# Gate chunks of the in-projection in pairs by seven quarter products, their tanh through DRAM, projections by output feature

## Chip, cores and metric

One core of one Trainium2 chip. The metric is the device time of one launch in microseconds (us): 1536.8 us, the median of 3 runs (1535.43 to 1537.21).

## What is computed

Two layers of a decoder trunk over 1024 prompt rows and 8 sample rows, 1032 in all. Cut to what matters here, each layer does, in fp32:

```
h = x @ w_in                          # (1032, 1024) @ (1024, 5632)
xa, za, u, v, zb, q, k, vv, zc, gates = split(h)
ya = pool_mix(xa) * silu(za)          # 256 features
yb = u * sgu(layer_norm(v)) * silu(zb)   # 256
yc = window_attention(rope(q), rope(k), vv) * silu(zc)   # 512
merged = sum over i of sigmoid(gates_i + b_gate_i) * (y_i @ w_proj_i)   # i = a, b, c; 1024 each
x = layer_norm(ALPHA * x + merged @ w_out)
```

Every product is made of three fp32r products of high and low parts: x_h w_h + x_l w_h + x_h w_l.

## The kernel before

x lies in SBUF by feature as XH and XL (8 slices of 128 features by 1032 rows). A chunk is 128 output features of the in-projection. `unit(w, s)` (line 584) makes a third of a chunk (384, 384 or 264 rows): 8 slices by 3 terms, 24 matmuls into one of 4 PSUM banks (`acc`). What follows reads that bank: tanh on ScalarE (ACT), arithmetic on VectorE (DVE). The weights of the next chunk are loaded by SP and split meanwhile (`prep_chunk`, line 184): ACT copies the high part `wh`, DVE subtracts the low part `wl` (`split`, lines 92 to 94).

The order within a layer is written out in lines 920 to 996: rows of v (`a0`), five rotary chunks (`rope`), chunks 0 to 3 of the pool branch (`b_chunk`), eight gate chunks of branch a (`c_chunk(0, d)`), chunks 4 to 11 (branch b, and four chunks of the attention's gate zc), eight gate chunks each of b and c, then the output projection with layer norm by blocks of rows (`d_mm`, `d_ln`, `d_tr`). In a `c_chunk` the projection of its branch is done right there, by `merge` (line 753): for each third it multiplies y and w_proj into a bank of `att`, and DVE makes `(tanh + 1) * product` and adds it to `mg[d]`. Each third's merge comes one unit after its gate.

The attention is cut into steps (`att_query`, `att_scores`, `att_norm`, `att_tr`, `att_pv`) that a list hands out between matmuls: `Jobs.pump` (line 48) is called every six matmuls, and starts a step that uses TensorE at most every 1.45 calls.

Each engine runs its own instructions in the order in which the program issues them, and an instruction that waits holds up those behind it.

Of the kernel before, what the change touches and what calls it, by code (L numbers as in the profile page):

```python
# [16 lines left out]
L = 2  # L17
S = 1024
# [9 lines left out]
class Jobs:  # L28
    def __init__(self):
        self.tick = 0  # L30
        self.lists = [deque(), deque(), deque()]
        self.at = {}
        self.free = 0
# [13 lines left out]

    def pump(self):
        self.tick += 1
        for i in (0, 2, 1):  # L50
            q = self.lists[i]
            while q and all(k in self.at and self.tick >= self.at[k] + lag for k, lag in q[0][2]):
                if i == 1 and self.tick < self.free:
                    break
                if self._run(q):
                    if i == 1:
                        self.free = max(self.free, self.tick - 1) + 1.45
                    return

# [10 lines left out]
class Feed:  # L70
    """Raw weights, loaded in the order in which they are split."""

    def __init__(self, nc, new, items, first=()):
        self.nc, self.new, self.items, self.raw = nc, new, deque(items), deque()
        self.first = deque(first)

    def stage(self):
        if self.items:
            src = self.items.popleft()
            n = src.free_size()  # L80
            t = self.first.popleft() if self.first else self.new()
            self.nc.sync.dma_start(out=t[:, 0:n], in_=src)
            self.raw.append((t, n))

    def take(self, use, stage=True):
        t, n = self.raw.popleft()
        use(t[:, 0:n])
        if stage:
            self.stage()
# [8 lines left out]
def trunk_kernel(  # L98
    ctx: ExitStack,
    tc: tile.TileContext,  # L100
    xb, xs, xp, xst, wA, wB, wC, wP, wPc, wO, lcol, lrow, kcT, ck, cv, hist, ln, tab, c_a, c_b,
# [8 lines left out]
    wrp = ctx.enter_context(tc.tile_pool(name="wrp", bufs=2))  # L110
    wlp = ctx.enter_context(tc.tile_pool(name="wlp", bufs=2))
    whp = ctx.enter_context(tc.tile_pool(name="whp", bufs=2))
    prp = ctx.enter_context(tc.tile_pool(name="prp", bufs=1))
    plp = ctx.enter_context(tc.tile_pool(name="plp", bufs=2))
    php = ctx.enter_context(tc.tile_pool(name="php", bufs=2))
# [6 lines left out]

    def t_acc():
        return acc.tile([128, 512], F32, tag="acc", name="acc")
# [4 lines left out]
    def t_w2():  # L129
        return w2.tile([128, 512], F32, tag="w2", name="w2")  # L130
# [4 lines left out]
    def t_m(j, dt=F32R, name="m", n=T):  # L135
        return big.tile([128, n], dt, tag=f"m{j}", name=f"{name}{j}")
# [3 lines left out]

    def t_q(j, dt=F32R, n=T, name="q"):
        return big.tile([128, n], dt, tag=f"q{j}", name=f"{name}{j}")

    def t_r(j, dt=F32R, n=T, name="r"):
        return big.tile([128, n], dt, tag=f"r{j}", name=f"{name}{j}")
# [5 lines left out]
    x2d.append(drm.tile([NS, DM], F32, name="x2ds"))  # L151

# [9 lines left out]
    def order():  # L162
        for l in range(L):
            yield from [wA[l, :, k:k + 2] for k in (0, 2, 4, 6)]
            yield from [wB[l, j] for j in range(9)]
            yield from [wC[l, 0, d] for d in range(8)]
            yield from [wB[l, j] for j in range(9, 17)]
            yield from [wC[l, 1, d] for d in range(8)]
            yield from [wC[l, 2, d] for d in range(5)]
            yield wO[l, 0, :, 0:2]  # L170
            yield wC[l, 2, 5]
            yield wO[l, 0, :, 2:4]
            yield from [wC[l, 2, d] for d in range(6, 8)]
            yield from [wO[l, 0, :, k:k + 2] for k in (4, 6)]
            yield from [wO[l, 1, :, k:k + 2] for k in (0, 2, 4, 6)]

    def proj_order():
        for l in range(L):
            yield from [wP[l, i, d] for i in range(2) for d in range(4)]
            yield from [wPc[l, d] for d in range(8)]  # L180

    wq, pq_, half_done = deque(), deque(), []

    def prep_chunk(m=None, parts=2):
        """Splits the next raw chunk, or one half of it."""
        if not half_done:
            raw, n = feed.raw.popleft()
            if m is None:
                h = whp.tile([128, 1024], F32R, tag="wh", name="wh")
                lo = wlp.tile([128, 1024], F32R, tag="wl", name="wl")  # L190
            else:
                h, lo = [t_m(m + i, name="wm")[:, 0:1024] for i in range(2)]
            half_done.append((h, lo, raw))
            wq.append((h, lo))
            cs = slice(0, 1024 if parts == 2 else 512)
        else:
            h, lo, raw = half_done[0]
            cs = slice(512, 1024)
        split(nc, h[:, cs], lo[:, cs], raw[:, cs])
        if cs.stop == 1024:  # L200
            half_done.pop()
            feed.stage()

    def prep_proj():
        def use(raw):
            h = php.tile([128, 512], F32R, tag="ph", name="ph")
            lo = plp.tile([128, 512], F32R, tag="pl", name="pl")
            split(nc, h, lo, raw)
            pq_.append((h, lo))
        if pfeed.raw:  # L210
            pfeed.take(use)

    class Slices:
        """One group of columns of a weight of 1024 rows: per 128 rows, its high and its low part."""

        def __init__(self, where, cols=512):
            self.h, self.lo, self.n, self.where, self.cols = {}, {}, 0, where, cols

        def prep(self, n=4, stage=True):
            for _ in range(n):  # L220
                if self.n < 4:
                    feed.take(self._pair, stage)

        def _pair(self, raw):
            k0, n = 2 * self.n, self.cols
            if self.where == "p" and k0 == 0:
                self.p = t_p(name="slp")
            if self.where == "p" and k0 >= 4:
                h = whp.tile([128, 1024], F32R, tag="wh", name="slh")[:, 0:2 * n]
                lo = wlp.tile([128, 1024], F32R, tag="wl", name="sll")[:, 0:2 * n]  # L230
                split(nc, h, lo, raw)
                for j in range(2):
                    self.h[k0 + j], self.lo[k0 + j] = h[:, j * n:j * n + n], lo[:, j * n:j * n + n]
            else:
                for j in range(2):
                    k = k0 + j
# [75 lines left out]
    class Layer:  # L312
# [38 lines left out]
        def rope(self, j):  # L351
            w = wq.popleft()
            cos, sin = self.tab
            for s in range(3):
                p, e, n = self.unit(w, s)
                if s < 2 and j != 1:
                    prep_chunk(parts=1)
# [243 lines left out]
        def b_chunk(self, j):  # L601
            w = wq.popleft()
            for s in range(3):
# [15 lines left out]
                if s < 2:  # L619
                    prep_chunk(parts=1)  # L620
# [480 lines left out]
```

## Time and profile before

| | |
|---|---|
| median of 3 runs | 1536.8 us |
| span of the profiled execution | 1535.0 us (the three runs lie 0.4 to 2.2 us above it) |
| TensorE matmul (PE) busy | 1514.7 us, 99% |
| VectorE (DVE) | 733.3 us, 48% |
| ScalarE (ACT) | 494.9 us, 32% |
| GpSimd (POOL) | 212.3 us, 14% |
| DMA | 63 GB/s on average, 96.65 MB |

The page shows the span of one execution; its own time outside the span isn't shown. Matmuls are pipelined: one of 384 columns is shown as some 340 ns, while the next starts 175 ns after it. So the steps between starts, and not the durations, make up the time of TensorE.

### The profile page before, as it was taken

Reading aid. Unit: us, or ns where it says so; the run is one execution under the profiler, and the core shown is the slowest. Engines: PE = TensorE matmul, PEld = TensorE weight load, DVE = VectorE, ACT = ScalarE, POOL = GpSimd, SP = SyncE. Lnnn points to the kernel's source line nnn. Section 1 sums busy time; section 2 is a strip of 40 time slices with the busy share of each in tenths; the row PEclk is TensorE's granted clock in tenths of the full one; section 3 lists DMA queues with packets and bytes.
Section 4 is the critical chain, followed back from the end, with each engine's and each line's share of the span. In section 5 each row is a group of like instructions: output and inputs, shape, how many; then the busy total and the mean of one; then the engine's idle time right before and its main releaser. Section 6 shows DMA issues by size and latency. Waiting matters only on the chain.

```text
span 1535.0 us, 23080 instructions
## 1 busy us (share of the span) xinstructions
PE 1514.7 (99%) x9344; PEld 1432.1 (93%) x9344; DVE 733.3 (48%) x1726; ACT 494.9 (32%) x1163; POOL 212.3 (14%) x300
## 2 busy tenths in 40 slices
PE   8999999999999999999999999999999999999997
PEld 8998899999999999988799988999999999999876
DVE  6347755424433333364863477554243333332647
ACT  4454555421222212140215545554212222122300
POOL 4523110000000000001565231100000000000015
PEclk9999999999999999999999999999999999999999
DMA  6311111111111112233413111111111111121313
GB/s 228 114 52 31 35 44 35 35 49 32 52 50 42 48 44 67 62 104 97 139 69 128 47 36 30 37 34 42 42 42 42 56 49 35 56 63 49 120 59 124
DMA packets 43418, 96.65 MB, mean 63 GB/s; under 512 B 8864, under 2 KB 14032, under 8 KB 43280
## 3 DMA queue, kind: packets, MB, share of 16 engines
q1 hardware_dynamic: 33232, 86.16, 17.4%
q10 hardware_dynamic: 10080, 9.03, 1.7%
q8 instruction: 73, 1.20, 0.3%
q14 instruction: 33, 0.27, 0.1%
HBM read 86.14 MB, written 11.11 MB: 63 GB/s over the span
## 4 chain that ended last, share of the span: by engine, by line
PE 46%; DVE 3%; ACT 1%; issue 0%; POOL 0%; DVEq 0%; POOLq 0%; ACTq 0%
PE acc L591 29%; PE acc L295 7%; PE att L761 6%; PE att L489 1%; PE att L448 1%; PE att L478 1%; PE acc L301 1%; ACT w L456 0%; DVE w L468 0%; PE att L720 0%; DVE rr L839 0%; DVE rr L842 0%; DVE sll L94 0%; POOL rr L843 0%; DVE py L690 0%
## 5 line engine op out<-in xcount | busy, mean ns | idle before, releaser
L591 PE MATMUL acc<-XH,wh 128*128 128x384 f32 (+1 forms) x1872 | 611.9, 327 | 0.0
L591 PE MATMUL acc<-XL,wh 128*128 128x384 f32 (+1 forms) x1872 | 598.5, 320 | 0.0
L591 PE MATMUL acc<-XH,wl 128*128 128x384 f32 (+1 forms) x1872 | 598.5, 320 | 0.0
L591 PEld LDWEIGHTS acc<-XH,wh 128*128 128x128 f32 x1872 | 352.4, 188 | 14.0 <-issue 12.5
L591 PEld LDWEIGHTS acc<-XL,wh 128*128 128x128 f32 x1872 | 352.7, 188 | 1.2
L591 PEld LDWEIGHTS acc<-XH,wl 128*128 128x128 f32 x1872 | 352.1, 188 | 0.0
L94 DVE TENSOR_TENSOR wl<-wr,wh 128x512 fp32r<-128x512 f32 x156 | 109.2, 700 | 289.1 <-ACT wh L93 288.8
L776 ACT ACTIVATE w<-acc,halves 128x384 f32<-128x384 f32 x144 | 78.5, 545 | 411.2 <-PE acc L591 411.2
L284 POOL TENSOR_TENSOR rr<-rr,mhalf 128x1 f32<-128x1 f32 (+1 forms) x18 | 10.3, 572 | 959.7 <-DVE rr L283 959.7
L93 ACT ACTIVATE wh<-wr 128x512 fp32r<-128x512 f32 x156 | 97.0, 624 | 27.0 <-PE acc L591 19.5
L456 ACT ACTIVATE w<-w,ns 128x256 f32<-128x256 f32 (+1 forms) x128 | 62.4, 488 | 116.9 <-DVE ns L454 116.9
L295 PE MATMUL acc<-slp,XH 128*128 128x384 f32 (+1 forms) x256 | 73.7, 371 | 5.8 <-ACT slp L93 5.8
L765 DVE SCALAR_TENSOR_TENSOR w<-w,att 128x384 f32<-128x384 f32 (+1 forms) x96 | 48.9, 510 | 37.6 <-PE att L761 37.6
L361 ACT ACTIVATE w<-acc 32x384 f32<-32x384 f32 (+1 forms) x120 | 53.9, 449 | 36.1 <-PE acc L591 33.3
L761 PE MATMUL att<-ycl,ph 128*128 128x384 f32 (+1 forms) x192 | 61.5, 320 | 0.0
L761 PE MATMUL att<-ych,pl 128*128 128x384 f32 (+1 forms) x192 | 61.4, 320 | 0.0
L761 PE MATMUL att<-ych,ph 128*128 128x384 f32 (+1 forms) x192 | 61.2, 319 | 0.0
L295 PEld LDWEIGHTS acc<-slp,XH 128*128 128x128 f32 x256 | 47.9, 192 | 11.7 <-ACT slp L93 5.8
L454 DVE CUSTOM_DVE_ANT_0 w<-att,cb,skn 128x256 f32<-128x256 f32 (+1 forms) x128 | 54.7, 465 | 8.6 <-PE att L448 6.8
L94 DVE TENSOR_TENSOR pl<-pr,ph 128x512 fp32r<-128x512 f32 x32 | 22.1, 692 | 68.3 <-ACT ph L93 68.3
L598 ACT ACTIVATE w<-acc 128x384 f32<-128x384 f32 (+1 forms) x48 | 21.8, 455 | 93.9 <-PE acc L591 93.9
L766 DVE TENSOR_TENSOR mg<-mg,w 128x384 f32<-128x384 f32 (+1 forms) x96 | 49.6, 516 | 3.3
(205 smaller groups left out, 2241.8 us busy)
## 6 DMA issues: line engine op xcount, KB each, us to landing
wr<-in_wC_dram SPq DMA_DIRECT2D x48, 512.0 KB
wr<-in_wB_dram SPq DMA_DIRECT2D x34, 512.0 KB
wr<-in_wO_dram SPq DMA_DIRECT2D x16, 512.0 KB
pr<-in_wP_dram SPq DMA_DIRECT2D x16, 256.0 KB
pr<-in_wPc_dram SPq DMA_DIRECT2D x16, 256.0 KB
w<-in_xp_dram SPq DMA_DIRECT2D x16, 256.0 KB
x2d<-rr ACTq DMA_DIRECT2D x16, 256.0 KB
w<-x2d SPq DMA_DIRECT2D x16, 256.0 KB
```

The costliest lines, as they stand in the source:

```text
L93: nc.scalar.activation(h, raw, AF.Copy)
L94: nc.vector.tensor_tensor(lo, raw, h.bitcast(F32), op=ALU.subtract)
L295: PE.matmul(p[:, 0:n], x[:, k, blk(b)], c, start=(i == 0 and j == 0), stop=(i == len(terms) - 1 and j == len(t) - 1))
L361: A.activation(t[a:a + 32, 0:n], p[b:b + 32], AF.Copy)
L454: V.tensor_tensor_reduce(o, ps[:, i * 256:i * 256 + w], mask[:, m0:m0 + w], 1.0, self.c["skn"][:, j:j + 1], op0=ALU.add, op1=ALU.min, accu ...
L456: A.activation(o, o, AF.Exp, bias=nm[:, i:i + 1], scale=-1.0, accum_out=su[:, i:i + 1])
L591: PE.matmul(p[:, 0:n], a[:, c], b[:, k, o:o + n], start=(k == 0 and j == 0), stop=(k == 7 and j == 2))
L598: A.activation(t[:, 0:n], p, AF.Tanh, scale=0.5)
L761: PE.matmul(q[:, 0:n], a[:, c], b[:, e], start=(k == 0 and j == 0), stop=(k == nk - 1 and j == 2))
L765: V.scalar_tensor_tensor(t[:, 0:n], t[:, 0:n], 1.0, q[:, 0:n], op0=ALU.add, op1=ALU.mult)
L766: V.tensor_tensor(m[:, e], m[:, e], t[:, 0:n], op=ALU.add)
L776: A.activation(t[:, 0:n], p, AF.Tanh, bias=self.c["h"][:, i * 8 + d:i * 8 + d + 1], scale=0.5)
```

## The change

**Products.** The 24 gate chunks and the 4 zc chunks are made in 14 pairs per layer (`pair`). The 1024 input features, the 256 output features of a pair and the 1032 rows are each cut in two halves, and the pair is seven products (the Winograd form of Strassen) of 512 features by 128 outputs by 516 rows, where eight would be the plain way. A product is 4 slices by 3 terms by 2 matmuls of 258 columns. The sums that it needs:

- of weights: 4 additions of 128 by 512 per pair on POOL (`first`, `second`);
- of x: T2, T3 and T4 of four slices each, by 44 additions of 128 by 516 per layer on POOL, and each of the 12 slices is split again by ACT and DVE (`queue_folds`, a fourth list of jobs, one per pump in which no TensorE step starts); a last sum overwrites half of XH and XL after chunk 7 (`fold_last`);
- of products: PSUM accumulates some, ACT makes one copy and DVE six additions of 516 per pair.

**Order.** Chunks 0 to 7 come first, then 12 gate pairs, 2 zc pairs, and then all projections (`project(d)`, for output features d = 0 to 7). The tanh of the gates goes to DRAM and comes back (`gd`), as do ya and yb (`yd`). All of y is split into high and low parts after the last pair.

**Buffers.** PSUM `acc` is 2 pairs of banks. Weight tiles are half as large (512 columns) and more (`wr` 6, `wh` and `wl` 4). The scratch tiles `w2` are 4 where they were 8, with 4 `ap` for the attention. The pace of attention steps is 2.6 calls.

The core of the diff:

```diff
-    w2 = ctx.enter_context(tc.tile_pool(name="w2", bufs=8))
-    acc = ctx.enter_context(tc.tile_pool(name="acc", bufs=4, space=PSUM))
+    stp = ctx.enter_context(tc.tile_pool(name="stp", bufs=3))
+    w2 = ctx.enter_context(tc.tile_pool(name="w2", bufs=4))
+    app = ctx.enter_context(tc.tile_pool(name="app", bufs=4))
+    acc = ctx.enter_context(tc.tile_pool(name="acc", bufs=2, space=PSUM))
...
+        def fold(self, k0, k1, dst, eng):
+            (a, ao), (b, bo) = k1, k0
+            h, lo = [t_st() if eng is None else t_w2()[:, 0:HT] for _ in range(2)]
+            eng = eng or G
+            eng.tensor_tensor(h, XH[:, a, ao:ao + HT].bitcast(F32), XH[:, b, bo:bo + HT].bitcast(F32), op=ALU.subtract)
+            eng.tensor_tensor(lo, XL[:, a, ao:ao + HT].bitcast(F32), XL[:, b, bo:bo + HT].bitcast(F32), op=ALU.subtract)
+            eng.tensor_tensor(dst, h, lo, op=ALU.add)
...
+            def t3(k):
+                r = t_st()
+                self.fold((k, HT), (k + 4, HT), r, None)
+                split(nc, *place(3, k), r)
+                return False
...
+            for k in range(4):
+                J.add(3, lambda k=k: t3(k), ("T3", k), [(("pool", 1), 2)])
+            for k in range(4):
+                J.add(3, lambda k=k: t2(k), ("T2", k))
+            for k in range(4):
+                J.add(3, lambda k=k: t4(k), ("T4", k), [(("ya", 1), 6)])
+
+        def fold_last(self):
+            for k in range(4):
+                r = t_w2()[:, 0:HT]
+                self.fold((k, 0), (k, HT), r, V if k % 2 else G)
+                split(nc, XH[:, k, HT:T], XL[:, k, HT:T], r)
...
+        def product(self, n, ps, first):
+            h, lo = ready.popleft()
+            for k in range(4):
+                c = slice(k * 128, k * 128 + 128)
+                xh, xl = self.quarter(n, k)
+                for j, (a, b) in enumerate(((h, xh), (h, xl), (lo, xh))):
+                    for s in range(2):
+                        PE.matmul(ps[:, s, 0:258], a[:, c], b[:, s * 258:s * 258 + 258],
...
+            A_, B_ = t_two(), t_two()
+            self.product(11, A_, True)
+            A.activation(v(lo1), ps(A_), AF.Copy)
+            self.product(2, B_, True)
+            add(hi0, lo1, B_)
+            self.product(21, A_, False)
+            use(0, 0, ps(A_))
+            self.product(3, B_, False)
+            add(hi1, lo1, B_)
+            C_ = t_two()
+            self.product(1, C_, True)
+            add(hi1, hi1, C_)
+            use(1, 1, v(hi1))
+            self.product(4, B_, False)
+            add(lo1, lo1, B_)
+            use(1, 0, v(lo1))
+            self.product(22, C_, False)
+            add(hi0, hi0, C_)
+            use(0, 1, v(hi0))
...
+                for q in range(2):
+                    ps = t_two()
...
+                    V.scalar_tensor_tensor(v(t), v(t), 1.0, ps[:, :, 0:258], op0=ALU.add, op1=ALU.mult)
+                    if i:
+                        (V if last else G).tensor_tensor(m[:, e], m[:, e], t[:, e], op=ALU.add)
+                    if i == 2:
+                        split(nc, XH[:, d, e], XL[:, d, e], m[:, e])
+                    if (i < 2 and q) or (i == 2 and not q and d >= 3):
+                        prep()
```

What this does to the order of instructions is shown at three places.

**ScalarE while x is summed** (layer 0, chunks 3 and 4). L598 and L615 are the tanh of a unit's bank, L93 and L94 the copies of high parts (of weights `wh`, of ya `yah`, of T3 and T2), L427 and L445 the attention's query, L456 and L474 its exponentials, L480 and L498 its copy of transposed rows. Before:

```order
L598 ACTIVATE w_1700<-acc 128x264 [waits PE_49]
L495 ACTIVATE yc<-att 128x4x128 [waits PE_49]
L480 ACTIVATE w_1740<-att 128x512 [waits PE_49]
L598 ACTIVATE w_1748<-acc 128x384 [waits PE_49]
L93 ACTIVATE wh<-wr 128x512 [waits DMAHW3_49]
L427 ACTIVATE ks_688<-yc 64x256
L456 ACTIVATE w_1765,ns<-w_1765,ns 128x256 [waits DVE_49] x2
L459 ACTIVATE ns<-ns 128x2 [waits DVE_49]
```

And now:

```order
L615 ACTIVATE w_1872<-acc 128x384 [waits PE_49]
L94 ACTIVATE wh<-wr 128x512 [waits DMAHW0_49]
L651 DMA yd_108<-yax_1155 128x1032 [waits DMAHW2_49,DVE_49]
L94 ACTIVATE T3x_1894<-st 128x516 [waits Pool_49]
L498 ACTIVATE ap<-att 128x512 [waits PE_49]
L94 ACTIVATE T3x_1894<-st 128x516 [waits Pool_49]
L94 ACTIVATE T2x_1943<-st 128x516 [waits Pool_49]
L615 ACTIVATE w_1947<-acc 128x384 [waits DVE_49,PE_49]
L94 ACTIVATE wh<-wr 128x512
L445 ACTIVATE ksu_734<-yc 64x256
L474 ACTIVATE ap,ns<-ap,ns 128x256 [waits DVE_49] x2
L477 ACTIVATE ns<-ns 128x2 [waits DVE_49]
L94 ACTIVATE T2x_1943<-st 128x516 [waits Pool_49]
L498 ACTIVATE ap<-att 128x512 [waits PE_49]
```

The copies of T3 and T2, each behind a wait for POOL, stand between the tanh of a unit and the attention's copies.

**ScalarE at the first pair** (layer 0). Before, at the end of chunk 3 and the first gate chunk (L776 is the gate's tanh):

```order
L93 ACTIVATE yah_1910<-ya_1109 128x384 [waits DVE_49,PE_49,Pool_49]
L93 ACTIVATE yah_1910<-ya_1109 128x384 [waits DVE_49]
L93 ACTIVATE yah_1910<-ya_1109 128x264 [waits DVE_49]
L480 ACTIVATE w_1936<-att 128x512 [waits PE_49]
L776 ACTIVATE w_1938<-acc,halves 128x384
L93 ACTIVATE wh<-wr 128x512 [waits DMAHW6_49]
L427 ACTIVATE ks_688<-yc 64x256
```

Now, from the end of chunk 7 (L651 sends yb to DRAM, the four L94 with `XH` are `fold_last`, L821 is the copy of product 11 which product 21 waits for):

```order
L651 DMA yd_110<-ybu_1832 128x1032 [waits DVE_49]
L94 ACTIVATE XH<-w_2560 128x516 [waits Pool_49]
L94 ACTIVATE XH<-w_2568 128x516 [waits DVE_49]
L94 ACTIVATE XH<-w_2576 128x516 [waits Pool_49]
L94 ACTIVATE XH<-w_2584 128x516 [waits DVE_49]
L94 ACTIVATE wh<-wr 128x512 [waits DMAHW6_49]
L498 ACTIVATE ap<-att 128x512 [waits PE_49]
L94 ACTIVATE wh<-wr 128x512
L445 ACTIVATE ksu_734<-yc 64x256
L474 ACTIVATE ap,ns<-ap,ns 128x256 [waits DVE_49] x2
L477 ACTIVATE ns<-ns 128x2 [waits DVE_49]
L821 ACTIVATE gu_2593<-acc 128x516 [waits PE_49]
```

The four copies of `fold_last` come first, in turns with POOL and DVE; the third weight tile of the pair and then the copy of product 11 stand behind them.

**VectorE in the projections** (layer 1 before, chunk by chunk; layer 0 now, d = 2). L763 to L766 and L907 multiply a product with its gate or add it up. Before:

```order
L765 SCALAR_TENSOR_TENSOR w_11838<-w_11838,att 128x384 [waits PE_49]
L766 TENSOR_TENSOR mg_9799<-mg_9799,w_11838 128x384 [waits DVE_49]
L94 TENSOR_TENSOR pl<-pr,ph 128x512 [waits DMAHW0_49,Activation_49]
L765 SCALAR_TENSOR_TENSOR w_11869<-w_11869,att 128x384 [waits PE_49]
L766 TENSOR_TENSOR mg_9799<-mg_9799,w_11869 128x384 [waits DVE_49]
L765 SCALAR_TENSOR_TENSOR w_11909<-w_11909,att 128x264 [waits PE_49]
L766 TENSOR_TENSOR mg_9799<-mg_9799,w_11909 128x264 [waits DVE_49]
```

Now:

```order
L907 SCALAR_TENSOR_TENSOR glu_6543<-glu_6543,acc 128x516 [waits DMAHW2_49,PE_49]
L907 SCALAR_TENSOR_TENSOR glu_6543<-glu_6543,acc 128x516 [waits PE_49]
L95 TENSOR_TENSOR wl<-wr,wh 128x512 [waits Activation_49]
L907 SCALAR_TENSOR_TENSOR glu_6615<-glu_6615,acc 128x516 [waits DMAHW5_49,DVE_49,PE_49]
L907 SCALAR_TENSOR_TENSOR glu_6615<-glu_6615,acc 128x516 [waits PE_49]
L95 TENSOR_TENSOR wl<-wr,wh 128x512 [waits Activation_49]
L907 SCALAR_TENSOR_TENSOR glu_6675<-glu_6675,acc 128x516 [waits DMAHW6_49,DVE_49,PE_49]
L95 TENSOR_TENSOR XL<-glu_6543,XH 128x516 [waits Activation_49]
L907 SCALAR_TENSOR_TENSOR glu_6675<-glu_6675,acc 128x516 [waits PE_49]
L95 TENSOR_TENSOR XL<-glu_6543,XH 128x516 [waits Activation_49]
```

The additions into `mg` have gone to POOL, and the split of XL, which waits for ACT and so for POOL, stands between the readers of two banks (rows 7 and 9) and ahead of those of the next d.

## Rows read from the trace of the kernel before

**Rows 1.** The page: span, busy time of the engines, clock in 40 slices.

```profile
span 1535.0 us, 23080 instructions
PE 1514.7 (99%) x9344; PEld 1432.1 (93%) x9344; DVE 733.3 (48%) x1726; ACT 494.9 (32%) x1163; POOL 212.3 (14%) x300
PEclk9999999999999999999999999999999999999999
```

**Rows 2.** Waits of TensorE, the longest: line, waited for; us in all, times, longest.

```profile
PE acc L295 <- ACT slp L93: 5.8, 1, 5.8
```

**Rows 3.** Chain that ended last: start, us, units of two gate chunks.

```profile
1237.97 8.41 PE acc L591 x48
1247.44 2.90 PE acc L591 x24
```

**Rows 4.** Timeline, TensorE: start, us; weight loads (PEld) and attention steps.

```profile
402.35 0.19 PEld L591 LDWEIGHTS acc<-XH,wl 128*128 128x128 f32 x1
...
206.56 0.60 PE L478 MATMUL att<-ident,w 128*128 128x128 f32 x4
206.91 0.37 PE L591 MATMUL acc<-XH,wh 128*128 128x264 f32 x1
...
207.73 0.64 PE L448 MATMUL att<-ks 128*128 128x256 f32 x4
208.20 0.29 PE L591 MATMUL acc<-XH,wh 128*128 128x264 f32 x1
```

**Rows 5.** Timeline, POOL: two-input additions of several widths.

```profile
91.07 1.01 POOL L364 TENSOR_TENSOR yc<-yc,w 128x384 f32<-128x384 f32 x1 [2.87 <-DVE w L363]
104.65 0.76 POOL L364 TENSOR_TENSOR yc<-yc,w 128x264 f32<-128x264 f32 x1 [1.25 <-DVE w L363]
137.28 1.89 POOL L666 TENSOR_TENSOR px<-xa 128x1024 f32<-128x1024 f32 x1
...
729.44 3.81 POOL L843 TENSOR_TENSOR rr<-rr,w 128x512 f32<-128x512 f32 x2 [1.77 <-issue]
735.53 2.87 POOL L843 TENSOR_TENSOR rr<-rr,w 128x512 f32<-128x512 f32 x2 [1.77 <-issue]
```

**Rows 6.** Groups by form, DVE, ACT and POOL: busy us, mean ns, idle before.

```profile
L94 DVE TENSOR_TENSOR wl<-wr,wh 128x512 fp32r<-128x512 f32 x156 | 109.2, 700 | 289.1 <-ACT wh L93 288.8
...
L94 DVE TENSOR_TENSOR ycl<-yc,ych 128x1032 fp32r<-128x1032 f32 x8 | 9.7, 1230 | 4.7 <-ACT ych L93 4.7
...
L93 ACT ACTIVATE wh<-wr 128x512 fp32r<-128x512 f32 x156 | 97.0, 624 | 27.0 <-PE acc L591 19.5 <-POOL vns L339 7.1
L93 ACT ACTIVATE ych<-yc 128x1032 fp32r<-128x1032 f32 x8 | 8.3, 1063 | 5.8 <-DVE yc L618 4.0 <-PE att L761 1.9
...
L420 POOL TENSOR_TENSOR ks<-kT,ks 64x128 fp32r<-64x128 f32 x64 | 32.6, 509 | 4.3
L418 POOL CAST ks<-kT 64x128 fp32r<-64x128 f32 x64 | 20.6, 322 | 170.6 <-PE att L448 168.1
```

**Rows 7.** Windows of the first 20 us: PE, PEld, DVE, ACT, POOL busy, clock, DMA, GB/s.

```profile
0.00:5.00 5.00, 0.00 (x0) 0.00 (x0) 0.38 (x2) 1.91 (x2) 0.20 (x4) 1.00 0.60 167
5.00:10.00 5.00, 4.15 (x12) 3.79 (x13) 4.35 (x7) 4.16 (x8) 0.00 (x0) 1.00 1.03 386
10.00:15.00 5.00, 5.00 (x26) 5.00 (x25) 3.02 (x7) 2.35 (x4) 0.55 (x1) 1.00 1.03 389
15.00:20.00 5.00, 5.00 (x30) 5.00 (x30) 3.23 (x10) 1.46 (x3) 3.20 (x4) 1.00 1.03 419
```

**Rows 8.** Timeline, TensorE, the first block of rows.

```profile
10.45 0.52 PE L295 MATMUL acc<-sll,XH 128*128 128x384 f32 x1
10.77 0.52 PE L295 MATMUL acc<-slh,XL 128*128 128x384 f32 x1
...
11.68 0.34 PE L295 MATMUL acc<-slh,XL 128*128 128x384 f32 x1
11.86 0.33 PE L295 MATMUL acc<-slh,XH 128*128 128x384 f32 x1
```

More of the change, by code (lines that the diff above doesn't have):

```diff
@@ L17 @@
 L = 2
+HT = 516
 S = 1024
@@ L46, in _run, with _ready @@
         return pe is not False
+    def _ready(self, q):
+        return q and all(k in self.at and self.tick >= self.at[k] + lag for k, lag in q[0][2])
     def pump(self):
@@ L51, in pump @@
             q = self.lists[i]
-            while q and all(k in self.at and self.tick >= self.at[k] + lag for k, lag in q[0][2]):
+            while self._ready(q):
                 if i == 1 and self.tick < self.free:
@@ L70, with __init__, stage @@
 class Feed:
-    def __init__(self, nc, new, items, first=()):
+    def __init__(self, nc, new, items):
         self.nc, self.new, self.items, self.raw = nc, new, deque(items), deque()
[L75 to L89, printed above, removed]
+    def stage(self, n=1):
+        for _ in range(n):
+            if self.items:
+                src = self.items.popleft()
+                c = src.free_size()
+                t = self.new()[:, 0:c]
+                self.nc.sync.dma_start(out=t, in_=src)
+                self.raw.append(t)
 def split(nc, h, lo, raw):
@@ L121, in trunk_kernel, with t_two @@
     ctx.enter_context(tc.manual_schedule())
+    half = []
+    def t_two():
+        return acc.tile([128, 2, 512], F32, tag="acc", name="acc")
     def t_acc():
-        return acc.tile([128, 512], F32, tag="acc", name="acc")
+        if not half:
+            t = t_two()
+            half.extend([t[:, 1], t[:, 0]])
+        return half.pop()
     def t_att():
@@ L151, in trunk_kernel @@
     x2d.append(drm.tile([NS, DM], F32, name="x2ds"))
+    yd = [[drm.tile([128, T], F32, name=f"yd{i}{j}") for j in range(2)] for i in range(2)]
+    gd = [[drm.tile([128, T], F32, name=f"gd{i}{d}") for d in range(8)] for i in range(3)]
     def row_bcast(src, n, parts=128):
@@ L174, in order @@
[L174 to L190, printed above, removed]
-            else:
[L192 to L211, printed above, removed]
+            yield from [wA[l, :, k] for k in range(8)]
+            yield from [wB[l, j, :, 4 * h:4 * h + 4] for j in range(13) for h in range(2)]
+            yield from [wS[l, p, q] for p in range(14) for q in range(4)]
@@ L213, in trunk_kernel, with __init__, prep @@
     class Slices:
-        def __init__(self, where, cols=512):
-            self.h, self.lo, self.n, self.where, self.cols = {}, {}, 0, where, cols
-        def prep(self, n=4, stage=True):
+        def __init__(self, slots, cols=512):
+            self.h, self.lo, self.slots, self.cols = {}, {}, slots, cols
+        def prep(self, n=1):
             for _ in range(n):
[L221 to L236, printed above, removed]
-                    t = self.p[:, k, :] if self.where == "p" else t_q(k, name="slq") if k < 4 else t_r(k - 4, name="slr")
-                    self.h[k], self.lo[k] = t[:, 0:n], t[:, 512:512 + n]
-                    split(nc, self.h[k], self.lo[k], raw[:, j * n:j * n + n])
-            self.n += 1
```

514 lines of the change are left out of this document (296 added, 218 removed).

## Prediction

> **What bounds the kernel now.** I read the page first: TensorE is busy 99% of the span, at the full clock in each of 40 slices, while DVE is at 48%, ACT at 32% and POOL at 14% [rows 1]. The reader is to see that nothing but TensorE's own work sets the time. The waits say the same: TensorE's idle time is 1535.0 - 1514.7 = 20.3 us in all [rows 1], of which 5.8 is the start [rows 2], while DVE waits 288.8 us for copies of weights alone [rows 6]. The chain of waits is one long run of matmuls: 48 of 384 columns in 8.41 us (0.175 each), 24 of 264 in 2.90 (0.121) [rows 3]. 0.175/384 and 0.121/264 are both 0.46 ns a column, so the time goes by columns. A weight load takes 0.19 us, longer than the 0.121 from matmul to matmul [rows 3, 4], and still a 264-column matmul isn't held up by it; 258 columns will not be either. So what the change takes from TensorE is a gain, and each wait that it gives TensorE is a loss in full.
>
> **The gain.** A chunk is 8.41 + 2.90 = 11.31 us [rows 3]; 28 per layer, 56 in all, go: 633 us. In their place stand 28 pairs of 7 products of 24 matmuls with 258 columns, 0.118 each by columns: 2.84 us a product, 19.9 a pair, 557 us. **-76 us** (with 0.117 to 0.119: -71 to -81). The projections have the same columns as before. Everything else depends on whether TensorE is kept going: acc has two pairs of banks now, so a product starts only when the last but one has been read.
>
> **A. Sums of x during chunks 4 to 7.** POOL does 44 additions of 516 columns per layer. A two-input addition takes it 1.01 us with 384 columns and 0.76 with 264, 0.0021 a column, so 1.30 with 516; one of 1024 in 1.89 would make it 0.98; two of 512 took 2.87 and 3.81, 1.43 to 1.9 each, beside a busy DVE [rows 5]. I take 1.30, worked from the nearest widths, with 0.98 and 1.5 as bounds. The order shows ACT's copies of these sums, each waiting for POOL, between the tanh of units and the copies of the attention. Counted from the start of chunk 3's last unit: the copy of T3(2) stands behind a tanh at 9.0, T3(3) is summed by about 13.2. Then POOL alone does 30 more up to the third T4: T2(0) 5 x 1.30 = 6.5, a block of keys (four casts of 0.32 and four additions of 0.51 [rows 6]) 3.3, T2(1) to T2(3) 19.5, three T4 11.7: 41.0 in all, to 54.2. ACT's copy, DVE's subtraction and the attention's norm behind it (0.65, 0.7, 1.2, as copies and subtractions of 512 take [rows 6]) end at 56.8. TensorE reaches the transposes that need this norm, ahead of chunk 6, after units of 2.9 + 8.4 + 2.9 + 8.4 + 2.9 = 25.5 [rows 3] and some twelve steps of attention and mixing at 0.35 to 0.47 [rows 4], about 5.4: 30.9. It waits **25.9 us** (by 0.98: 16; by 1.5: 32).
>
> In a sentence apart: the Trainium skill, "GPSIMD Engine Reference", section 3.1, has 4497 ns for an addition of 2048 fp32 elements, by which 516 would take an estimated 1.13 us and A come to some 21; rows 5 don't scale as its single ratio does, and I keep 1.30.
>
> **B. `fold_last` after chunk 7.** Four sums, each of three additions, then a copy (ACT) and a subtraction (DVE). Only four `w2` tiles: the next sum needs those of the last one. POOL and DVE take turns, and ACT takes the four copies in order. With 1.30 (POOL) and 0.7 (DVE and ACT, [rows 6]) the four end 2.4, 6.0, 11.5 and 15.0 us after chunk 7. Behind them in ACT's order (shown above) stand the pair's third weight tile, the attention's copy, query and exponentials, and then the copy of product 11: at about 21. Product 21 adds to that bank and could have started at 6.8 (two products and steps of attention [rows 4]). **14.2 us** (9 to 16).
>
> **C. From the last product to d = 0.** DVE finishes the pair (4.3 us), then ACT and DVE split eight rows of y, of which the last four alone are late before but here all are issued there: 1.06 and 1.23 us each [rows 6]; they end at 14.2. Only behind them does DVE read the first bank. The projection's six units have two pairs of banks, so units 3 to 6 start at 15.0, 16.4, 17.8 and 20.6, and d = 0 ends at 23.5 where 11.3 of matmuls would do. **12.2 us** (10 to 15).
>
> **D. d = 1 to 7.** Per d TensorE has four units of 1.42 and two of 2.84 us. DVE's order (shown above) has, behind the sixth unit's reader, the split of XL: it waits for the fifth's chain, which is reader on DVE 0.7, addition on POOL 1.30, copy on ACT 0.62; then the same for the sixth [rows 5, 6]. So DVE is free for the next d only 4.5 us after the last matmul, 5.2 where a weight tile stands there too (d from 3). Unit 3 of the next d, which needs the first reader's bank, starts at 5.3 (6.0) instead of 2.84: 2.43 us lost three times, 3.13 four times. **19.8 us** (14 to 24).
>
> **E. Pairs.** In a pair's 19.9 us POOL makes four sums of weights, 5.2; ACT seven copies of weights, one of a product and four tanh, twelve by some 0.65, 7.8; DVE seven subtractions and six additions by 0.7, 9.1 [rows 5, 6]. The attention comes on top for ACT and DVE, as it does before, where they idle more than half the time [rows 1]. All is less than TensorE's time, but in order and with one product of slack: **1 us** (0 to 8). The tanh's trips to DRAM, 24 of 0.53 MB out and back per layer, I cost at nothing: the DMA moves 63 GB/s on average and has done 419 [rows 7], and they are due a hundred us later.
>
> **F. Start, once.** By the order, SP issues the last two weight tiles of the first rows behind all of x: 6.4 MB. With 0.83, 1.9, 1.9 and 2.1 MB in the first four stretches of 5 us [rows 7] they land near 19 us, split by 20. TensorE reached them at about 12 (the 16 matmuls with `slp` before them, 0.32 apart [rows 8], then 0.175 [rows 3]). **8 us** (5 to 11).
>
> **G. Clock.** The first matmuls of 384 columns start 0.32 us apart [rows 8], the pace of the 1.2 GHz level, after TensorE had been idle for 5.8 us [rows 2]; from 11.7 us on they start some 0.18 apart, the 2.4 GHz level, while the page's granted clock shows 9 (of ten) throughout [rows 1, 7]. In the 5.8 us between, 18 matmuls each lost 0.145: 2.6. New waits of 12 us and more may cost that again: I take one each layer, **2.6 us** (0 to 10, four of them).
>
> **The sum.** Per layer 25.9 + 14.2 + 12.2 + 19.8 + 1 + 2.6 = 75.7, twice 151.4; with 8 and -76 it is +83. The profiled span is 1535.0, so 1618; the median lies 1.8 above it: **1620 us**. Low bounds everywhere: 49 x 2 + 5 - 81 = +22, 1559; high bounds: 105 x 2 + 11 - 71 = +150, 1687. The terms hardly err all low at once; E, the least known, can only add. So the case's own range is 1565 to 1685.
>
> **Rivals.**
> *All waits covered.* The sums may land in time if ACT and DVE, which mostly idle [rows 1, 2], run ahead of what I count. Then only the gain and some start remain: 1537 - 76 = **1461**. For it: 99% of TensorE's time was kept through much the same attention. Against it: chain A is 30 additions of one engine in a row, and no other engine has them. Chance 0.09.
> *Half.* Overlap that I don't see halves A to D: 36 x 2 + 4 - 76 = 0, so **1537** (1510 to 1565): two products in flight would do it where DVE's waits are short. For it: I take each wait at its end in full. Against it: A to D stand at four places that don't help each other. Chance 0.12, of which faster 0.05, same 0.02, slower 0.05.
> *Clock.* TensorE may stay at the lower level in d = 1 to 7, with stops of 2 to 3 us in 14. Then a d takes 11.3 x 0.32/0.175 = 20.7 instead of 14.0 us: +6.7 x 14 = +94, **1715**. It decides when stops come this often; for it speak 18 slow matmuls after one idle stretch [rows 8], against it that no other wait of the profile shows such a slowing. Beside it: the Trainium skill, "TensorE: Matmul & The Clock Gate", part 1, says that an idle array falls back to 1.2 GHz; by that rule G and this rival would both be real, and rows 8 agree only for the start. Chance 0.06.
> *Not what it says.* The order has 7 x 24 matmuls of 258 columns per pair, so this is out.
>
> **How the numbers follow.** The forecast case has 0.73 and is slower throughout. Together: faster by over 0.2% (about what a measurement of this kernel can tell from no change) 0.09 + 0.05 = 0.14; same 0.02; slower 0.73 + 0.05 + 0.06 = 0.84. The range, 1555 to 1685, holds nearly all of the forecast case and a little of "half"; left out are the covered case, most of "half" and the clock, 0.2 in all.
>
> **What would show it.** A product's 24 matmuls in 2.84 us. A: TensorE waits some 26 us for an attention step in chunks 4 to 6, POOL busy without a gap before it. B: one wait of 14 us before product 21 of the first pair. C and D: waits for DVE's reader in each d, its split of XL waiting for ACT. F: a gap of 8 us near 12. The forecast falls if POOL's additions take under 0.8 us, if those waits belong to an engine that isn't on the chain, or if pairs take over 24 us with TensorE waiting in each: then E is the term.

## The result: 1824.4 us, 19% slower

The changed kernel takes 1824.4 us (median of 4 runs, 1817.6 to 1829.8) where the kernel before takes 1536.2: a ratio of 1.187, 95% interval 1.184 to 1.190. The forecast was 1620, with a range up to 1685. The sign is right, the size is not: 288 us came where 83 were expected.

The page of the changed kernel, beside [rows 1]:

```profile
span 1828.0 us, 26460 instructions
...
PE 1538.5 (84%) x10400; PEld 1428.7 (78%) x10400; DVE 928.8 (51%) x1830; ACT 575.5 (31%) x1239; POOL 578.7 (32%) x568
...
PEclk7989987999999998999999999788999999999999
```

TensorE's idle time has gone from 20.3 to 1828.0 - 1538.5 = 289.5 us, and the granted clock, 9 in each slice before, falls to 7 and 8 in eight of the 40. Over the span its mean went from 0.997 to 0.939. The clock has two levels, so (1 - 0.939) x 2 = 12% of the span, some 220 us in 34 stretches, was at the lower one, 1.2 GHz. In the trace TensorE was at work for 136 us of these, which at the full clock would have taken 68. Before, that loss was 2 us. So the 293 us between the two spans are 269 of new waiting, 66 of lower clock, and only 42 less work instead of the 76 that were to go.

The largest waits of TensorE, beside the single one of [rows 2] (line, waited for; us in all, times, longest):

```profile
PE acc L608 <- DVE ybu L616: 67.3, 6, 22.4
PE acc L905 <- DVE glu L907: 34.2, 22, 3.6
PE acc L608 <- DVE yc L383: 31.8, 12, 3.1
PE acc L316 <- DVE vnu L358: 22.1, 8, 4.3
PE att L496 <- DVE ap L486: 20.4, 6, 8.1
PE acc L608 <- DVE yax L616: 13.3, 6, 3.5
PE acc L608 <- DVE ybu L630: 11.3, 6, 2.3
PE acc L316 <- ACT slx L94: 10.7, 1, 10.7
...
PE acc L801 <- ACT gu L821: 10.1, 6, 2.7
```

The reader is to see lines that no term of the prediction names: L316 (rows of v), and L608 behind L383 (rotary chunks). The change left the arithmetic of those stages as it was. Their weights come in smaller tiles now, but what the waits name is the bank, and that comes from `t_acc`.

### The profile page after: what moved, and what is told of

Its sections match the earlier page's. It is cut to its first block, busy times and chain, and to the rows that moved or that the text cites. A ratio compares the mean times of both kernels' runs of the same rounds, so it can differ in the third digit from the quotient of the medians.

```text
span 1828.0 us, 26460 instructions
## 1 busy us (share of the span) xinstructions
PE 1538.5 (84%) x10400; PEld 1428.7 (78%) x10400; DVE 928.8 (51%) x1830; ACT 575.5 (31%) x1239; POOL 578.7 (32%) x568
## 5 line engine op out<-in xcount | busy, mean ns | idle before, releaser
L608 PE MATMUL acc<-XH,wh 128*128 128x384 f32 (+1 forms) x624 | 223.8, 359 | 137.3 <-DVE ybu L616 67.3
L608 PEld LDWEIGHTS acc<-XH,wh 128*128 128x128 f32 x624 | 128.7, 206 | 155.7 <-DVE ybu L616 69.3
L95 DVE TENSOR_TENSOR wl<-wr,wh 128x512 fp32r<-128x512 f32 x196 | 155.1, 791 | 111.4 <-ACT wh L94 111.3
L608 PE MATMUL acc<-XL,wh 128*128 128x384 f32 (+1 forms) x624 | 211.1, 338 | 0.0
L608 PE MATMUL acc<-XH,wl 128*128 128x384 f32 (+1 forms) x624 | 211.0, 338 | 0.0
L801 PE MATMUL acc<-XH,wh 128*128 128x258 f32 x896 | 185.2, 288 | 11.0 <-ACT gu L821 10.1
L801 PE MATMUL acc<-XL,wh 128*128 128x258 f32 x896 | 183.8, 287 | 0.0
L801 PE MATMUL acc<-XH,wl 128*128 128x258 f32 x896 | 182.9, 286 | 0.0
L94 ACT ACTIVATE wh<-wr 128x512 fp32r<-128x512 f32 x196 | 122.9, 627 | 108.4 <-PE acc L801 51.8
L801 PEld LDWEIGHTS acc<-XH,wh 128*128 128x128 f32 x896 | 140.6, 192 | 15.6 <-ACT gu L821 11.7
L801 PEld LDWEIGHTS acc<-XH,wl 128*128 128x128 f32 x896 | 140.7, 192 | 0.8 <-issue 0.8
L316 PE MATMUL acc<-slx,XH 128*128 128x512 f32 (+1 forms) x384 | 118.1, 391 | 21.5 <-ACT slx L94 10.7
L905 PE MATMUL acc<-yhx,wh 128*128 128x258 f32 x512 | 93.6, 308 | 43.0 <-DVE glu L907 34.2
L608 PEld LDWEIGHTS acc<-XL,wh 128*128 128x128 f32 x624 | 128.5, 206 | 1.1
L608 PEld LDWEIGHTS acc<-XH,wl 128*128 128x128 f32 x624 | 127.9, 205 | 0.0
L474 ACT ACTIVATE ap<-ap,ns 128x256 f32<-128x256 f32 (+1 forms) x128 | 62.4, 488 | 169.0 <-DVE ns L472 169.0
L316 PE MATMUL acc<-slp,XH 128*128 128x384 f32 (+1 forms) x256 | 82.9, 409 | 37.6 <-DVE vnu L358 22.1
L95 DVE TENSOR_TENSOR wl<-st,wh 128x512 fp32r<-128x512 f32 x84 | 58.1, 691 | 96.9 <-ACT wh L94 96.9
```

Source lines behind the costliest of these rows:

```text
L94: nc.scalar.activation(h, raw, AF.Copy)
L95: nc.vector.tensor_tensor(lo, raw, h.bitcast(F32), op=ALU.subtract)
L316: PE.matmul(p[:, 0:n], x[:, k, blk(b)], c, start=(i == 0 and j == 0), stop=(i == len(terms) - 1 and j == len(t) - 1))
L474: A.activation(o, o, AF.Exp, bias=nm[:, i:i + 1], scale=-1.0, accum_out=su[:, i:i + 1])
L608: PE.matmul(p[:, 0:n], a[:, c], b[:, k, o:o + n], start=(k == 0 and j == 0), stop=(k == 7 and j == 2))
L801: PE.matmul(ps[:, s, 0:258], a[:, c], b[:, s * 258:s * 258 + 258], start=(first and k == 0 and j == 0), stop=(k == 3 and j == 2), skip_gro ...
```

## Where the unforeseen waits come from

The first rotary chunk shows one. TensorE, ACT and DVE, in order of start (start us, us, what, and idle time with what ended it):

```profile
85.47 0.34 PE L608 MATMUL acc<-XH,wl 128*128 128x384 f32 x1
85.84 1.96 ACT L382 ACTIVATE w<-acc 32x384 f32<-32x384 f32 x4 [2.24 <-PE acc L608]
87.84 0.56 DVE L383 TENSOR_TENSOR kTu<-acc,tabx 128x384 f32<-128x384 f32 x1 [3.18 <-ACT w L382]
88.45 0.39 PE L608 MATMUL acc<-XH,wh 128*128 128x264 f32 x1 [2.64 <-DVE kTu L383]
```

A unit ends at 85.8, ACT and DVE read its bank until 88.4, and only then does the next unit start, though it writes to another bank. One unit earlier the same readers held nobody up. `t_acc` hands out the two halves of a pair in turn:

```
def t_acc():
    if not half:
        t = t_two()
        half.extend([t[:, 1], t[:, 0]])
    return half.pop()
```

Counted through the program, it is always the second half that waits, and for the readers of the first: 384 rows after 384, 264 after 384, 384 after 264, whatever the stage. Theory "halves": the two banks of a pair are one tile, and the second unit is made to wait for the first one's reader. Theory "depth": two pairs in flight instead of four banks are too few. The first experiment tells them apart, since it gives up the second bank and so has still fewer units in flight.

## The experiments

**1. Each unit a pair of its own.**

```diff
-        if not half:
-            t = t_two()
-            half.extend([t[:, 1], t[:, 0]])
-        return half.pop()
+        return t_two()[:, 0]
```

> Each unit gets a pair of banks of its own (its second bank unused) instead of one half of a pair. Theory 'halves': in the changed kernel the second unit of a pair of banks waits for the reader of the first, a wait that the bank itself does not need; then the waits of TensorE for DVE L358, L383, L623, L616 (yax), L630 and L326, 95 us in all, go, and with them the stretches at the lower clock behind them (some 25 by 3.4 us at half pace, 43 us): about 1824 - 138 = 1686 us (1660 to 1740). Rival 'depth': the waits come from having only two pairs in flight; then fewer units in flight make it no better: 1820 us or more.

Measured: 1676.2 us, 148 less than the changed kernel (ratio to before 1.090, 1.087 to 1.094). The waits that are left:

```profile
PE acc L605 <- DVE ybu L613: 35.7, 8, 6.4
PE acc L902 <- DVE glu L904: 34.1, 22, 3.6
PE att L493 <- DVE ap L483: 30.1, 8, 8.1
PE acc L313 <- ACT slx L94: 12.1, 1, 12.1
...
PE acc L605 <- DVE yc L380: 3.2, 2, 1.7
...
PE acc L313 <- DVE vnu L355: 0.7, 2, 0.5
```

(The edit moves the lines up by three.) The wait for L383, now L380, went from 31.8 to 3.2, that for L358, now L355, from 22.1 to 0.7. "Depth" is out: with half the banks in use the waits are gone.

**2. The same pairing in the kernel before.** If it is the pairing, it must cost without any of the rest.

```diff
-    acc = ctx.enter_context(tc.tile_pool(name="acc", bufs=4, space=PSUM))
+    acc = ctx.enter_context(tc.tile_pool(name="acc", bufs=2, space=PSUM))
...
-        return acc.tile([128, 512], F32, tag="acc", name="acc")
+        if not half:
+            t = acc.tile([128, 2, 512], F32, tag="acc", name="acc")
+            half.extend([t[:, 1], t[:, 0]])
+        return half.pop()
```

> The kernel before, with one edit: its four single banks for products become two pairs whose halves are handed out in turn, as in the changed kernel. If sharing a pair makes the second unit wait for the reader of the first whatever else the kernel does: the waits for DVE of the rows, the rotary chunks and chunks 0 to 7 appear as in the changed kernel (some 50 us a layer), those of the gate chunks for their tanh come on top (42 second halves a layer by 0.5 to 1 us), with the lower clock behind the longer ones: 1537 + 140 to 230, 1680 to 1770 us. If the waits of the changed kernel come from its other order, and not from the pairs: under 1560 us.

Measured: 1784.8 us (ratio 1.162, 1.158 to 1.165), 248 more, even above the expected 140 to 230. Its waits are those of the changed kernel, with the gates' tanh on top:

```profile
PE acc L596 <- ACT w L781: 34.0, 32, 2.2
PE acc L596 <- DVE yc L367: 30.3, 12, 2.7
PE acc L300 <- DVE vn L342: 22.0, 8, 4.3
```

Four single banks and two pairs of banks are the same storage, so the wait comes with making two banks one tile. It stands in the program: the first matmul of a second half has a wait for DVE or ACT that the single banks did not need.

**3. TensorE kept busy in those waits.** Ahead of a unit in a second half TensorE does ten matmuls for nothing.

```diff
+            fill(half)
             p = t_acc()
...
+    def fill(second):
+        if second:
+            ps = t_att()
+            for i in range(10):
+                PE.matmul(ps[:, 0:384], XH[:, 0, 0:128], XH[:, 0, 0:384], start=(i == 0), stop=(i == 9))
```

> The changed kernel, and ahead of every unit that takes the second half of a pair of banks (and of such a block of rows of v) TensorE does 10 matmuls of 384 columns (1.75 us at the higher clock) whose result nobody reads. The waits for the readers stay, but TensorE idles less in them. If the stretches at the lower clock come from that idling: fewer than 34 stretches, and less time although there is more work: 1824 - 30 (1775 to 1810). If the clock falls for another reason, or the fillers only add work: 1824 to 1900 us.

Measured: 1807.4 us, 17 less than the changed kernel, with 480 matmuls (10400 to 10880) more. The stretches at the lower clock fell from 34 to 17, and the page's PE line went up:

```profile
PE 1593.7 (88%) x10880; PEld 1486.6 (82%) x10880; DVE 926.9 (51%) x1830; ACT 575.5 (32%) x1239; POOL 579.9 (32%) x568
```

480 x 0.175 = 84 us of work was added, and the time fell. Most of the fillers went into what had been waits: the idle time fell from 289.5 to 1805.0 - 1593.7 = 211.3 us. That the time fell at all is the clock: the waits end when the readers are done, fillers or not, but TensorE was at work for 72 us at the lower clock where it had been for 136, which gives back 32. The saving is smaller than the 30 hoped for, but within its range.

**4. The sums of x left out** (term A). Products 2, 3 and 4 read plain quarters of x, and the sums are not made; nothing else is left out. The kernel then computes something else, and stands here for its time alone. Once on the changed kernel, and once on experiment 1:

```diff
-            if n in (2, 3, 4):
-                return [t[:, k % 2] for t in self.T[n, k - k % 2]]
-            r, o = {11: (0, 0), 21: (4, 0), 22: (4, HT), 1: (0, HT)}[n]
+            r, o = {2: (0, 0), 3: (4, 0), 4: (4, HT), 11: (0, 0), 21: (4, 0), 22: (4, HT), 1: (0, HT)}[n]
...
-            if j == 2:
-                y.queue_folds()
```

> Leaves out the 12 sums T2, T3, T4 per layer (44 additions on POOL, 12 copies on ACT, 12 subtractions on DVE); products 2, 3 and 4 read plain quarters of x. Theory (term A of the prediction): the two long waits for DVE L616 in chunks 4 and 5 (22.3 and 11.2 us) and the stretches of 23.9 and 13.7 us at the lower clock behind them, some 52 us a layer, go: about 1720 us (1700 to 1745). Rival: those waits only show the sharing of a pair of banks, and POOL's sums are not behind them: a loss of under 20 us, over 1800 us.

> The first two edits together: units with a pair of banks each, and the sums T2, T3, T4 left out. Theory: what is left of term A in the first run, waits of some 55 us (DVE ybu, ap, ACT ap) and 34 us lost at the lower clock behind them, goes: 1676 - 89 = 1587 us (1575 to 1605). Rival: with units alone the sums are mostly hidden: over 1640 us.

Measured: 1750.2 us, 74 less than the changed kernel (105 were expected), and 1599.5, 77 less than experiment 1 (89 expected). The 105 counted the slow stretches of 23.9 and 13.7 us at half their whole length; but TensorE was still waiting for 18.4 and 8.7 us of them. Only the 5.5 and 4.9 us behind the waits were work at half pace: 22.3 + 11.2 + 5.2 = 38.7 a layer, close to the 37 that came. Whether units share pairs or not, the sums cost 37 to 38 us a layer, lower clock included. The trace of the changed kernel shows the chain as the prediction had it: POOL without a gap (from 253 to 299 us), ACT behind it, TensorE behind ACT and so behind the DVE reader that ACT feeds (timeline of POOL, ACT and PE):

```profile
263.53 1.27 POOL L661 TENSOR_TENSOR st<-st 128x516 f32<-128x516 f32 x1
264.88 1.27 POOL L683 TENSOR_TENSOR st<-XH,st 128x516 f32<-128x516 f32 x1
...
274.49 0.63 ACT L94 ACTIVATE T2x<-st 128x516 fp32r<-128x516 f32 x1 [5.84 <-POOL st L684]
275.03 0.37 ACT L615 ACTIVATE w<-acc 128x264 f32<-128x264 f32 x1
...
276.63 0.69 PE L608 MATMUL acc<-XH,wh 128*128 128x384 f32 x1 [22.32 <-DVE ybu L616]
```

**5. The split of x in the projections one output feature later** (term D).

```diff
-                        split(nc, XH[:, d, e], XL[:, d, e], m[:, e])
+                        self.late.append((d, e, m))
...
+                if i == 0:
+                    self.split_late()
```

(The load of a later gate moves along with the split.)

> In the projections the split of XH and XL of output feature d is issued after the first two readers of d + 1. Theory (term D): DVE no longer stands before the split while ACT and POOL finish, the 1.73 us wait in each of d = 1 to 7 goes, with the slower matmuls behind it: 24 to 40 us in both layers, 1785 to 1800 us. Rival: TensorE waits there for POOL's additions or for two pairs of banks whatever the order: 1815 us or more.

Measured: 1791.8 us, 33 less, 16 a layer (its two runs lie 10 us apart, so this is known to some 10 us). TensorE's wait for L907 went from 34.2 us in 22 pieces to 12.0 in 14:

```profile
PE acc L905 <- DVE glu L907: 12.0, 14, 3.6
```

**6. `fold_last` taken apart** (term B), on top of experiment 1.

```diff
-        y.fold_last()
+        y.fold_last(0)
+        y.fold_last(1)
...
+                y.sum_last(0, G)
+                y.sum_last(1, V)
...
             A.activation(v(lo1), ps(A_), AF.Copy)
+            f(2)
             self.product(2, B_, True)
             add(hi0, lo1, B_)
+            f(3)
```

(`sum_last` makes the sum in one tile and without its split, during chunk 7; `f(k)` makes sum k on DVE with its split.)

> The first run's edit, and the four sums after chunk 7 taken apart: two are made during chunk 7 and split behind it, two are made on DVE between the products of the first pair. Theory (term B): the wait for the attention's norm (8.1 us a layer), the one for the copy of product 11 (2.7) and the 13.7 us at the lower clock behind them go: 1676 - 30 = 1646 us (1638 to 1660). Rival: the wait only moves to another product of the first pair: 1665 us or more.

Measured: 1666.0 us, 10 less where 30 were expected. The waits of 8.1 and 2.7 us are gone. But the sums now stand on DVE between the readers of the products, and TensorE waits 17.2 us in 16 pieces for those readers, where it waited 9.7 in 12:

```profile
PE acc L806 <- DVE gu L823: 17.2, 16, 2.3
```

Nor did the slow clock go: TensorE was at work for 87 us at the lower level in both. The rival (1665 us or more) was right.

**7. Edits together.** Experiments 1 and 5, the four sums on DVE between products, and the loads of x behind the weights of the first rows:

```diff
-    load_x(2)
-    load_layer(0)
...
     w0.prep(6)
+    load_x(2)
+    load_layer(0)
...
-        y.fold_last()
...
+            f(0)
             self.product(2, B_, True)
             add(hi0, lo1, B_)
+            f(1)
             self.product(21, A_, False)
             use(0, 0, ps(A_))
+            f(2)
             self.product(3, B_, False)
             add(hi1, lo1, B_)
+            f(3)
```

> Four edits at once: each unit a pair of banks of its own, the split of x in the projections one output feature later, the four sums after chunk 7 put between the products of the first pair (all on DVE), and the loads of x behind the eight weight slices of the first rows. If the waits add up with their slow stretches: 138 + 30 + 35 + 18 = 221 us less than 1824, 1603 us (1570 to 1640). If new waits take their place: 1680 us or more.

Measured: 1637.7 us, at the upper end of the first case. The sums of x, which this left as they were, still cost their 35.8 us of waits for L613. Then the odd sums of T2 and T4 on DVE, all with one tile and a later copy (`cut`):

```diff
-                split(nc, *place(2, k), r)
...
+                return run(V if k % 2 else G, r, [(XH[:, k, a], SUB, XH[:, k, b]), (ADD, XH[:, k + 4, b]), (ADD, XL[:, k, a]),
+                                                  (SUB, XL[:, k, b]), (ADD, XL[:, k + 4, b])])
...
+                    J.add(3, lambda m=m, q=q: cut(m, q), ("T%d" % m, q), [(("R%d" % m, q), 4)])
```

> The four edits of the fourth run, and the sums of x made in one tile each, the odd ones of T2 and T4 on DVE, with their copies issued four pumps after the sum. If POOL's row of additions is what holds up ACT and then TensorE: 1638 - 60 = 1578 us (1560 to 1600). If DVE is as late as POOL was: 1625 us or more.

Measured: 1609.3 us, 28 less where 60 were expected. DVE is late now, if not as late as POOL was: the 35.8 us for L613 fell to 1.2, and 13.7 came for DVE's query step (L443). The two slow each other down: DVE's timeline in the run that follows has

```profile
200.35 1.26 DVE L95 TENSOR_TENSOR wl<-wr,wh 128x512 fp32r<-128x512 f32 x1
201.54 1.79 DVE L679 TENSOR_TENSOR st<-XH 128x516 f32<-128x516 f32 x1
203.36 1.68 DVE L681 TENSOR_TENSOR st<-st,XH 128x516 f32<-128x516 f32 x1
205.08 4.05 DVE L681 TENSOR_TENSOR st<-st,XL 128x516 f32<-128x516 f32 x3
209.05 0.69 DVE L95 TENSOR_TENSOR T2x<-st,T2x 128x516 fp32r<-128x516 f32 x1
```

with POOL adding from 199.75 to 207.9, and a subtraction of 516 back at 0.69 once POOL has stopped. Then the splits of y moved into the last pair, and `fold_last` as in experiment 6:

```diff
-        y.split_y()
-        y.split_c()
+        y.split_c(1)
...
+        def last_pair(self, n):
+            for j in {4: (0, 1), 5: (2,), 6: (3,)}.get(n, ()):
+                self.split_y(j)
+            if n == 6:
+                self.split_c(0)
```

> As the run before, and: two of the four sums after chunk 7 are made during chunk 7; the rows of y are split between the products of the last pair; the loads of x start after two weight slices of the first rows. If B, C and F add up with the rest: 20 + 30 + 4 us less than the run before, some 1525 us (1510 to 1550), level with the kernel before or faster. If the splits between products hold up the pair's additions instead: 1560 us or more.

Measured: 1599.0 us (ratio 1.041, 1.038 to 1.044), the best of all, and still 62 over the kernel before: 10 less than the run before where 54 were expected. TensorE's wait for L443 grew from 13.7 us to 23.7, and 8.1 came at the start of the projections, where TensorE now waits for the last pair's additions on DVE, as the rival has it. Two further tries were slower than that. Three pairs of banks for products:

```diff
-    acc = ctx.enter_context(tc.tile_pool(name="acc", bufs=2, space=PSUM))
-    att = ctx.enter_context(tc.tile_pool(name="att", bufs=4, space=PSUM))
+    acc = ctx.enter_context(tc.tile_pool(name="acc", bufs=3, space=PSUM))
+    att = ctx.enter_context(tc.tile_pool(name="att", bufs=2, space=PSUM))
```

> As the run before with three pairs of banks for products and two banks for the attention (they were two and four). If TensorE's waits in the pairs (for DVE and ACT readers of gates, some 20 us) come from two pairs in flight: 10 to 25 us less than the run before. If two banks are too few for the attention: slower than the run before.

Measured: 1609.0 us. TensorE waits for the attention now (35.1 us for L469 ahead of the transposes); two banks are too few. And T4 later, all on POOL:

```diff
-                for n in (3, 2, 4):
+                for n in (3, 2):
                     for k in range(4):
                         J.need(("T%d" % n, k))
+                y.sum_last(1, V)
...
+            if k == 5:
+                self.jobs.need(("T4", 3))
```

> As the run with all edits (1599 us), with T4 left to POOL until product 4 of the first pair needs it, DVE's sums of T2 in two pieces, and the sums for the end of chunk 7 made ahead of chunks 6 and 7. If the crowd of sums ahead of chunk 7 was the cause of the wait for DVE L443 (11.8 us a layer) and of the slow stretch behind it: 1599 - 36 = 1563 us (1550 to 1580). If POOL is then late for product 4: 1590 us or more.

Measured: 1613.1 us. The wait of 11.8 us a layer is gone, but the first pair waits in other places: in layer 0 product 2 for DVE's reader of chunk 7 (4.3 us), product 21 for ACT's copy of product 11 (4.6) and product 1 for a tanh (2.8); the pairs take 343 us instead of 332. Product 4 itself started without a wait, so the time came out in the rival's range, but not for the rival's reason.

## Why the prediction was wrong, step by step

**The step that failed** is the last sentence under "The gain": "acc has two pairs of banks now, so a product starts only when the last but one has been read". It was applied to products and projections, which use whole pairs, and never to the units of the rows, rotary chunks and chunks 0 to 7, which use halves. There the rule is harsher: a unit in a second half starts only when the last one has been read. Undoing this alone gives back 148 of the 204 us between forecast and result. The order of the changed kernel had the sign of it. In the first rotary chunk the first matmuls of units wait for PE and for DVE by turns, where in the kernel before one unit after the other waits for ACT or DVE:

```
168 L608 MATMUL acc<-XH,wh 128x384 [waits PE_49]
192 L608 MATMUL acc<-XH,wh 128x264 [waits DVE_49]
216 L608 MATMUL acc<-XH,wh 128x384 [waits PE_49]
```

Units take turns in nothing but halves.

**G, the clock**, is the term that was most mis-sized: 2.6 us a layer against some 33. The mechanism was right, and so was the price of a stretch (34 of them, some 2 us each); the number of stretches was not: one a layer was counted, 17 came. From the last wait of term A (timeline of TensorE, 264 columns each):

```profile
301.72 0.42 PE L608 MATMUL acc<-XH,wl 128*128 128x264 f32 x1
301.94 0.42 PE L608 MATMUL acc<-XH,wh 128*128 128x264 f32 x1
...
326.08 0.28 PE L608 MATMUL acc<-XH,wh 128*128 128x264 f32 x1
326.20 0.28 PE L608 MATMUL acc<-XL,wh 128*128 128x264 f32 x1
```

0.22 us from start to start behind a wait of 11.2 us, 0.12 later on; the windows of the profile (us, busy time of PE, PEld, DVE, ACT and POOL, granted clock) put the clock beside it:

```profile
301.20:305.80 4.60, 4.60 (x21) 4.60 (x22) 1.67 (x5) 0.26 (x1) 0.83 (x3) 0.50 0.19 57
306.20:308.30 2.10, 2.10 (x17) 1.94 (x15) 1.10 (x5) 1.49 (x6) 0.31 (x1) 1.00 0.00 0
```

By the Trainium skill, "TensorE: Matmul & The Clock Gate", part 1, an idle array falls back to 1.2 GHz; the trace agrees (0.50 of the clock behind the wait of 11.2 us). The prediction counted only waits of 12 us and more, for which no row spoke. In layer 0 waits of 2.5 to 3.5 us, in rows, rotary chunks and chunk 3, were followed by such stretches in most cases (six of nine; a tenth came while the clock was still low). The rival "clock" had the right idea in the wrong place: in d = 1 to 7, with stops of 1.7 us, the clock fell once in layer 0.

**The gain** was -76 and came to 42 less work. A pair of matmuls with 258 columns starts every 0.243 us,

```profile
503.13 0.40 PE L801 MATMUL acc<-XL,wh 128*128 128x258 f32 x2
503.37 0.41 PE L801 MATMUL acc<-XH,wl 128*128 128x258 f32 x2
503.61 0.40 PE L801 MATMUL acc<-XH,wh 128*128 128x258 f32 x2
```

0.121 each and not 0.118: as long as one of 264 [rows 3]. "The time goes by columns" held from 264 to 384 and not at 258. Over 28 pairs that is 28 x 7 x 24 x 0.0033 = 15 us, and over the projections, 16 x 96 x 0.0033 = 5. The rest was not traced; part of it is that the page shows a matmul as busy some 0.17 us beyond the next one's start, which counts as work at each of the new waits.

**A** was 25.9 and measures 37 to 38 with its clock. POOL's price of an addition (mostly 1.27 to 1.30 us, up to 1.75), its unbroken row and the order of ACT's copies were as told. With halves TensorE stopped already at the next unit, 22.3 and 11.2 us. With units alone (experiment 1) its waits in chunks 4 to 6 of layer 0 are 5.9, 2.9, 6.4, 5.0 and 4.8, 25.0 in all, though in five places and not in one. The estimate by the Trainium skill, "GPSIMD Engine Reference", section 3.1, some 21, lies a little further from these 25.0 than the 25.9 did.

**B** was 14.2. TensorE waited 8.1 (for the norm) and 2.7 (for the copy of product 11), 10.8 a layer, with 13.7 us at the lower clock; taking it apart (experiment 6) gave back 5 a layer. The sums ended some 2, 7, 10 and 14 us after chunk 7, about as told, but the attention's norm held TensorE before the copy of product 11 did.

**C** was 12.2; the waits are 3.3, 1.1 and 3.6, 8.0. **D** was 19.8; the wait was 1.72 in each d where 2.43 to 3.13 were expected, 12 a layer, and experiment 5 gives 16 with the clock.

**E** was 1. In the pairs of layer 0 TensorE waited 18.5 us in all, 7.7 without the two waits of B: the upper end of its bounds.

**F** was 8: a wait of 10.7, and the rows of layer 0 end at 48.6 us with the loads of x behind eight weight slices (the first run of experiment 7) and at 43.1 with them behind two (the run of 1599.0), against 57.0 in experiment 1, clock included.

Three slips in its sums changed little: by its own prices the gain's bounds are -74 to -83, POOL's row up to the third T4 is 29 additions and not 30, and 1.89 us for 1024 columns makes 0.95 for 516.

So the forecast case had the sign, and TensorE does wait at the four places it named; there were as many more that it never looked at. The range, drawn from the bounds of the terms it had, could not hold a term it hadn't.

## What to carry to other kernels

When a change alters a buffer pool that many stages share, list every user of the pool, not only the new ones, and ask of each who must have read what before it may write; two buffers made one tile are waited for as one. Where an engine is the bound and has never idled, a wait of a few us costs itself and, on TensorE, some more in a slower clock behind it: here 66 us behind 269 of new waiting, and up to 3 behind a single wait of 2.6. A scheme that saves 4% of the bounding engine's work needs its additions to be free on the others: here the sums of x alone cost 74 to 77 us in two layers, more than the 62 that the products saved (56 chunks, 633 us, for 28 x 7 x 24 matmuls by 0.121, some 571).

## What was not expected of the hardware

- POOL and DVE slow each other when both add from SBUF: an addition of 516 on DVE took 1.35 to 1.79 us beside POOL's sums and 0.69 alone, one of POOL took up to 1.75 beside DVE and 1.27 alone, and two `tensor_scalar` of 256 columns took 2.66 us in the changed kernel's stretch of sums (0.62 at undisturbed places before). The mean of the weight subtraction L95 rose from 0.70 [rows 6] to 0.79. The Trainium skill, "SBUF — State Buffer", section "Who interferes with whom", says that DVE instructions with two inputs in SBUF, and `tensor_scalar` in its fast mode, contend with GpSimd for a shared port; the durations agree.
- Matmuls with 258 columns take as long as those with 264 (0.121 us from start to start). Why isn't shown.
- Work for nothing on TensorE made the kernel faster (experiment 3): 84 us of added matmuls, 17 us less in all.
